# Moving a form's sums to GpSimd and fetching its blocks ahead in a Strassen decoder layer

## The chip, the cores and the metric

The kernel runs on one core of one Trainium2 chip. The metric is the device time of one execution in microseconds (us); less is better.

## The reference

One decoder layer, batch 1, 512 positions, width 2048, all in float32. Cut to what matters:

```python
h = rmsnorm(x, attn_norm_g)
proj = h @ w_in                       # u, v_sgu, q, k, v_att, g_a, g_b
y_a = chunked_spatial_gating(gelu(u), rmsnorm(gelu(v_sgu)), w_s, b_s)
y_b = stick_breaking_attention(rmsnorm(q), rmsnorm(k), v_att)
x = x + (sigmoid(g_a) * (y_a @ w_up_a) + sigmoid(g_b) * (y_b @ w_up_b)) @ w_o
h = rmsnorm(x, ffn_norm_g)
gate, up = split(h @ w_ffn_in)
x = x + (silu(gate) * up) @ w_ffn_out
x = x + sigmoid(rmsnorm(x, ple_norm_g) @ w_ple_gate) * (p @ w_ple)
```

The products with the weights w_in, w_up, w_o, w_ffn_in, w_ffn_out and w_ple_gate are nearly all of the work.

## The kernel before

Activations are kept transposed, 128 rows of the width (the partitions) by 512 positions. A float32 operand is split in two parts, `hi` (rounded) and `lo` (the rest), and `mm3` multiplies hi by hi, hi by lo and lo by hi. A unit of work multiplies a square of the weights (256 by 256, as four 128x128 blocks) with a raw block of activations of 128x1024 (256 rows of the width). It does so plainly ("P") or by Strassen's seven products ("S"), which need sums of weight blocks and of activation blocks.

*Weights.* Each group is fetched by the DMA queue of SyncE (SP). For "S" an accumulating DMA issued by GpSimd (POOL) adds two blocks in memory (`landed`, L317). Then ScalarE (ACT) writes the high part (`whi`, L313) and VectorE (DVE) the low part (L310), into three slots. Up to eight groups are fetched ahead, into `landings` that the low split gives back.

*Forms.* A form is the split operand of one raw block: `parts` is the arena of the split operands, `wholes` the arena of raw blocks, sums and landed weights. `split_into` is an ACT instruction (L245) and then a DVE instruction (L246). A late form (`late_form`, `plain_first`) first makes four sums of 128x256 on DVE (L464), t0 from two blocks, t1 from t0, t2 from t1, and one more, then splits blocks 0 to 3 (128x1024), a tick later the three sums (128x768, "3x256" below), and after its plain use the last (128x256), which overwrites a block. There are 34 late forms: 8 of the first input x, 8 of the feed-forward's input x1, 13 of the hidden layer, 5 of the gate's input x2. A first pass uses a form plainly, and later passes use it by Strassen. Where a norm's gain belongs to a form, `gained` (L451, two ACT instructions) scales the raw block first. x1, the hidden layer and x2 are spilled to HBM and loaded again by `load` (L447).

*Order.* Each engine runs its instructions in order. `tick`, called after each unit, takes the first form from the queue `builds` when it is `ready` and there is room, and runs its first step, which begins with the load; its further steps run one tick each through `after`. Instructions issued in a tick stand behind the unit's own on engines that have such. POOL's instructions have no such place and are put where the scheduler finds room.

*First stage and norms.* `ple_operands` loads and splits pT, and three products with w_ple (`ple_pair`, L766 copies the banks out) run first. Then each of the eight blocks of x (xT, L783) is multiplied plainly by three units (`w_first`). `Norm` squares each block (L831 on ACT, L835 on DVE), and at the end a chain of steps makes the row of 1/rms: a matmul, a power on POOL (L852), `spread` (four small matmuls, L819, on diagonals that DVE makes, L817) and a copy.

## Time and profile before

| | us |
|---|---|
| median of 3 runs | 2727.55 (2724.98 to 2731.51) |
| the profiled execution's own time | 2727.38 |
| its span | 2725.7 |
| PE busy | 2691.7 (99%) |
| DVE busy | 2073.5 (76%) |
| ACT busy | 1353.6 (50%) |
| POOL busy | 444.3 (16%) |

The mean granted clock of TensorE (PE) was 0.996 of full speed. Busy times of different engines overlap and do not add up. Lines such as L464 are line numbers of the kernel before, also where the text speaks of the kernel after; only in the rows of the order below the kernel after has its own line numbers.

### The profile page before, as it was taken

The page shows a single profiled execution, that of the slowest core. Times are in us where ns is not written, and L with a number is a line of the kernel's source. Part 1 is how long each engine was busy: PE and PEld are TensorE (multiplying, and loading weights), DVE is VectorE, ACT ScalarE, POOL GpSimd, SP SyncE. Part 2 cuts the span into 40 slices and gives each one's busy share as a digit, 9 for nine tenths or more (in the row PEclk, how much of TensorE's full clock was granted, in tenths as well). Part 3 has the DMA queues.
Part 4 walks back from the last instruction along what each step waited for, and adds up shares of the span by engine and source line. Part 5 has one row for each costly group of instructions (what it writes and reads, how often), then busy time and mean ns, then how long its engine had stood idle before and what let it go on. Part 6 is the DMA issues. An engine that isn't in the chain of part 4 may idle for free.

```text
span 2725.7 us, 45769 instructions
## 1 busy us (share of the span) xinstructions
PE 2691.7 (99%) x17243; PEld 2442.4 (90%) x17243; DVE 2073.5 (76%) x3375; ACT 1353.6 (50%) x2043; POOL 444.3 (16%) x527
## 2 busy tenths in 40 slices
PE   8999999999999999999999999999999999999999
PEld 6899999999999889978888888888888998988898
DVE  7666767667777657668989898989898667778776
ACT  7655555555554334365444444444445344454543
POOL 0222223222220000001111111111111101111110
PEclk9999999999999999999999999999999999999999
DMA  7667676677776447767888878887887668788785
GB/s 220 157 175 172 174 177 170 166 174 191 172 193 207 135 138 203 199 206 200 210 205 199 209 201 206 203 202 204 204 199 211 178 179 237 197 251 237 224 222 156
DMA packets 302846, 529.05 MB, mean 194 GB/s; under 512 B 25632, under 2 KB 162848, under 8 KB 302624
## 3 DMA queue, kind: packets, MB, share of 16 engines
q1 hardware_dynamic: 241872, 425.70, 49.3%
q0 software_dynamic: 60752, 100.43, 23.6%
q8 instruction: 135, 2.21, 0.3%
q14 instruction: 87, 0.71, 0.1%
HBM read 478.84 MB, written 47.19 MB: 193 GB/s over the span
## 4 chain that ended last, share of the span: by engine, by line
PE 87%; DVE 5%; DMA 4%; ACT 2%; issue 1%; POOL 1%; SPq 0%; ACTq 0%; DVEq 0%; POOLq 0%
PE ps L251 18%; PE ps L252 18%; PE ps L250 18%; PE ps L589 17%; PE ps L591 9%; PE small L589 3%; DVE wlo L310 1%; PE small L591 1%; DMA wholes<-x 1%; DMA wholes<-w_ffn_out 1%; DVE parts L246 1%; DVE wholes L464 1%; PE small L1011 1%; PE small L987 1%; PE small L964 1%
## 5 line engine op out<-in xcount | busy, mean ns | idle before, releaser
L250 PE MATMUL ps<-parts,whi 128*128 128x256 f32 (+1 forms) x3995 | 1247.2, 314 | 19.4 <-ACT whi L313 10.8
L313 ACT ACTIVATE whi<-wholes 128x512 fp32r<-128x512 f32 (+4 forms) x950 | 855.6, 917 | 801.1 <-PE ps L251 330.5
L251 PE MATMUL ps<-parts,whi 128*128 128x256 f32 (+1 forms) x3960 | 1232.9, 311 | 3.0 <-DVE parts L246 3.0
L252 PE MATMUL ps<-parts,wlo 128*128 128x256 f32 (+1 forms) x3960 | 1231.1, 311 | 3.2 <-DVE wlo L310 3.0
L310 DVE TENSOR_TENSOR wlo<-wholes,whi 128x512 fp32r<-128x512 f32 (+4 forms) x950 | 964.4, 1048 | 147.1 <-ACT whi L313 145.8
L250 PEld LDWEIGHTS ps<-parts,whi 128*128 128x128 f32 x3995 | 763.9, 191 | 68.8 <-ACT whi L313 12.1
L251 PEld LDWEIGHTS ps<-parts,whi 128*128 128x128 f32 x3960 | 758.1, 191 | 49.0 <-DVE parts L246 6.2
L252 PEld LDWEIGHTS ps<-parts,wlo 128*128 128x128 f32 x3960 | 757.8, 191 | 42.9 <-DVE wlo L310 4.6
L589 PE MATMUL ps<-parts,whi 128*128 128x512 f32 x2064 | 725.3, 391 | 0.0
L591 PE MATMUL ps<-parts,wlo 128*128 128x256 f32 x2064 | 578.8, 280 | 0.0
L589 PEld LDWEIGHTS ps<-parts,whi 128*128 128x128 f32 x2064 | 386.7, 187 | 83.7
L591 PEld LDWEIGHTS ps<-parts,wlo 128*128 128x128 f32 x2064 | 390.3, 189 | 0.1
L329 DVE TENSOR_TENSOR wholes<-wholes 128x256 f32<-128x256 f32 (+1 forms) x794 | 328.0, 413 | 24.3 <-DMA wholes<-w_ffn_out 4.9
L317 POOL DMA_DIRECT2D wholes<-w_ffn_in x172 | 149.7, 871 | 746.2 <-DMA wholes<-w_ffn_in 246.0
L317 POOL DMA_DIRECT2D wholes<-w_in x132 | 118.7, 903 | 548.7 <-DMA wholes<-w_in 226.8
L649 DVE TENSOR_TENSOR out<-out,ps 128x256 f32<-128x256 f32 x258 | 107.3, 416 | 78.6 <-ACT out L646 78.6
L618 DVE TENSOR_TENSOR out<-out 128x256 f32<-128x256 f32 x59 | 25.0, 425 | 175.9 <-ACT out L615 175.6
L246 DVE TENSOR_TENSOR parts<-wholes,parts 128x1024 fp32r<-128x1024 f32 (+3 forms) x129 | 122.9, 963 | 23.5 <-ACT parts L245 23.3
L589 PE MATMUL small<-parts,whi 128*128 128x512 f32 x344 | 128.8, 391 | 0.0
L245 ACT ACTIVATE parts<-wholes 128x1024 fp32r<-128x1024 f32 (+3 forms) x129 | 105.8, 845 | 40.8 <-DMA wholes<-hid 16.9
L317 POOL DMA_DIRECT2D wholes<-w_ffn_out x56 | 57.0, 1034 | 404.7 <-DMA wholes<-w_ffn_out 181.2
L1256 ACT ACTIVATE out<-out 128x512 f32<-128x512 f32 x44 | 27.9, 633 | 167.0 <-DVE out L1255 167.0
(119 smaller groups left out, 1659.1 us busy)
## 6 DMA issues: line engine op xcount, KB each, us to landing
wholes<-w_ffn_in SPq DMA_DIRECT2D x172, 384.0 KB, 5.5
wholes<-w_in SPq DMA_DIRECT2D x132, 384.0 KB, 4.8
wholes<-w_ffn_in SPq DMA_DIRECT2D x172, 256.0 KB, 4.7
wholes<-w_ffn_in POOLq DMA_DIRECT2D x172, 256.0 KB, 5.3
wholes<-w_in SPq DMA_DIRECT2D x132, 256.0 KB, 4.0
wholes<-w_in POOLq DMA_DIRECT2D x132, 256.0 KB, 4.7
wholes<-x SPq DMA_DIRECT2D x32, 512.0 KB, 5.3
wholes<-w_ffn_out SPq DMA_DIRECT2D x31, 512.0 KB, 4.0
```

The costliest lines, as they stand in the source:

```text
L245: return (nc.scalar.activation(hi, src, AF.Copy), nc.vector.tensor_tensor(out=lo, in0=src, in1=hi.bitcast(F32), op=ALU.subtract))
L246: nc.vector.tensor_tensor(out=lo, in0=src, in1=hi.bitcast(F32), op=ALU.subtract))
L250: nc.tensor.matmul(ps[:, s], sh, mh[:, s], start=start, stop=False)
L251: nc.tensor.matmul(ps, sh, ml, start=False, stop=False)
L252: return nc.tensor.matmul(ps, sl, mh, start=False, stop=stop)
L310: in_turn(nc.vector.tensor_tensor(out=self.lo[:, blocks], in0=r, in1=h.bitcast(F32), op=ALU.subtract))
L313: in_turn(nc.scalar.activation(h, r, AF.Copy))
L317: nc.gpsimd.dma_start(out=raw[:, 3:5], in_=self.src[:, 1:3], accum_op=ALU.add)
L329: in_turn(nc.vector.tensor_tensor(out=o, in0=x, in1=y, op=ALU.add))
L589: nc.tensor.matmul(ps, wh[:, w], t[:, x].rearrange("p s c -> p (s c)"), start=first, stop=False)
L591: mark(nc.tensor.matmul(ps[:, :256], wl[:, w], t[:, x, 0], start=False, stop=last))
L649: in_turn(nc.vector.tensor_tensor(out=out, in0=x, in1=y, op=op))
```

## The change

Four things are done together.

1. `plain_first` issues the split of blocks 0 to 3 ahead of the four sums, and the sums on POOL instead of DVE.
2. A form of a spilled block (`far`) can have its raw block loaded before its turn: `tick` looks at the first three forms of `builds` (AHEAD), and a form is not begun until two ticks (WAIT) after its load was asked for. Loads take the place in `wholes` that was given back longest ago ("old").
3. A norm's chain starts by itself after its eighth block, and three ticks lie between the power and `spread`. The two lines that ran the second and third norm's chains are gone.
4. pT is loaded and split in two halves behind the first w_ple, and `ple_pair` runs over the halves in the outer loop, with both banks open.

```diff
+AHEAD, WAIT = 3, 2
...
         last, units = traced()[-1], dict(newest)
-        if builds and builds[0].ready() and fits(builds[0].sizes):
+        for f in list(builds)[:AHEAD]:
+            if not f.there and f.ready() and fits([(wholes, 1024, "old"), (wholes, 1024, "low")]):
+                f.fetch()
+                break
+        if builds and builds[0].ready() and builds[0].arrived() and fits(builds[0].sizes):
             builds.popleft().step()
...
+        def fetch(self):
+            self.block, self.there, self.due = self.src(), True, clock[0] + WAIT
+            self.sizes = self.sizes[:-1]
+
+        def arrived(self):
+            return self.there and clock[0] >= self.due
...
-        b, s, v = cut(raw.f()), take(768), take(256)
+        b, s, v = cut(raw.f()), take(768, "old"), take(256, "old")
         t, x = cut(s.f()), form.operand()
+        split_into(x[:, 0:4, 0], x[:, 0:4, 1], b)
         for out, p, q, op in ((t[:, 0], b[:, 1], b[:, 0], ALU.subtract),
                               (v.f(), b[:, 1], b[:, 3], ALU.subtract),
                               (t[:, 1], t[:, 0], b[:, 3], ALU.subtract),
                               (t[:, 2], t[:, 1], b[:, 2], ALU.add)):
-            nc.vector.tensor_tensor(out=out, in0=p, in1=q, op=op)
-        split_into(x[:, 0:4, 0], x[:, 0:4, 1], b)
+            nc.gpsimd.tensor_tensor(out=out, in0=p, in1=q, op=op)
...
-        raw = load(pT)
-        hi, lo = parts.take(1024, "high"), parts.take(1024, "high")
-        split_into(hi.own(), lo.own(), raw.f())
+        raw = take(1024, "old")
+        ps_p.extend(parts.take(1024, "high") for _ in range(2))
+        for k in (0, T):
+            nc.sync.dma_start(out=raw.f(k, k + T), in_=pT[:, k : k + T])
+            split_into(*(x.own(k, k + T) for x in ps_p), raw.f(k, k + T))
...
+    w_ple_0 = plain_weights(w_ple[0])
     ple_operands()
-    ple_pair(0, False)
+    ple_pair(0, w_ple_0)
...
                 self.chain = Staged(self.steps())
+                self.chain.go_on()
...
-            yield
+            for _ in range(3):
+                yield
             ps = spread(self.cols)
...
-    after(3, norm2.chain.step)
...
-    norm3.chain.step()
```

The DMA queue of SP at the start of the program, before: one load of pT, two blocks of xT, and the third block (the next L783) behind the first prefetches of w_in.

```order
L447 DMA wholes_74<-pT 128x1024
L293 DMA wholes_74<-w_ple 128x512
L789 DMA gcol_110<-gains 128x58
L293 DMA wholes_74<-w_ple 128x512 x2
L293 DMA wholes_74<-w_first 128x512
L783 DMA wholes_74<-xT 128x1024 x2
L293 DMA wholes_74<-w_first 128x512 x3
...
L295 DMA wholes_74<-w_in 128x2x256 x3
L783 DMA wholes_74<-xT 128x1024
L293 DMA wholes_74<-w_first 128x512 x2
L783 DMA wholes_74<-xT 128x1024
```

The same queue after (L314 is a weight load, L785 half of pT, L819 a block of xT):

```order
L314 DMA wholes_74<-w_ple 128x512
L785 DMA wholes_74<-pT 128x512 x2
L819 DMA wholes_74<-xT 128x1024
L826 DMA gcol_113<-gains 128x58
L314 DMA wholes_74<-w_ple 128x512 x2
L314 DMA wholes_74<-w_first 128x512
L819 DMA wholes_74<-xT 128x1024 x2
...
L314 DMA wholes_74<-w_first 128x512
L819 DMA wholes_74<-xT 128x1024 x2
L314 DMA wholes_74<-w_first 128x512 x2
L316 DMA wholes_74<-w_in 128x2x256
```

Three blocks of xT stand ahead of the first result's store, and five ahead of the first w_in.

ACT in the first stage, from the last high split of the first block of x on, before (L313 high splits, L245 splits of a form, L831 squares, L451 gains):

```order
L313 ACTIVATE whi2_80<-wholes_74 128x512
L245 ACTIVATE parts_73<-wholes_74 128x4x256
L831 ACTIVATE out_16_178<-wholes_74 128x1024
L313 ACTIVATE whi0_76<-wholes_74 128x512
L831 ACTIVATE out_19_204<-wholes_74 128x1024
L313 ACTIVATE whi1_78<-wholes_74 128x512
```

The same place after (L334 high splits, L266 splits of a form, L868 squares, L483 gains):

```order
L266 ACTIVATE parts_73<-wholes_74 128x4x256
L868 ACTIVATE out_16_181<-wholes_74 128x1024
L334 ACTIVATE whi2_80<-wholes_74 128x512
L483 ACTIVATE wholes_74<-wholes_74,gcol_113 128x512
L868 ACTIVATE out_21_209<-wholes_74 128x1024
L483 ACTIVATE wholes_74<-wholes_74,gcol_113 128x512
L868 ACTIVATE out_23_222<-wholes_74 128x1024
L266 ACTIVATE parts_73<-wholes_74 128x4x256
L334 ACTIVATE whi0_76<-wholes_74 128x512
L266 ACTIVATE parts_73<-wholes_74 128x3x256 x2
L334 ACTIVATE whi1_78<-wholes_74 128x512
```

The gains, the square and the split of the third block of x now stand ahead of whi0, the high split of the second block's first weights, and two splits of 3x256, which wait for POOL, ahead of whi1.

POOL from w_o to the first weights of w_ffn_out, before: it issues accumulating DMAs (L317) and one power.

```order
L317 DMA wholes_74<-w_o 128x512 x16
L317 DMA wholes_74<-w_ffn_in 128x512 x2
L852 TENSOR_TENSOR cols_918_11846<-mean_917_11844,expo_121 128x4
L317 DMA wholes_74<-w_ffn_in 128x512 x170
L317 DMA wholes_74<-w_ffn_out 128x512 x2
L317 DMA wholes_74<-w_ffn_out 128x2x128
```

The same stretch after, its last part (L338 accumulating DMAs, L497 sums):

```order
L338 DMA wholes_74<-w_ffn_in 128x512 x8
L497 TENSOR_TENSOR wholes_74<-wholes_74 128x256 x4
L338 DMA wholes_74<-w_ffn_in 128x512 x8
L497 TENSOR_TENSOR wholes_74<-wholes_74 128x256
L338 DMA wholes_74<-w_ffn_in 128x512 x136
L338 DMA wholes_74<-w_ffn_out 128x512
L497 TENSOR_TENSOR wholes_74<-wholes_74 128x256 x7
L338 DMA wholes_74<-w_ffn_out 128x512
L338 DMA wholes_74<-w_ffn_out 128x2x128
L497 TENSOR_TENSOR wholes_74<-wholes_74 128x256 x9
```

The sums of the first three hidden-layer forms stand among the DMAs of w_ffn_in, 136 of them ahead of the stage that uses them; the others follow the first DMA of w_ffn_out.

More of the change, by code (lines that the diff above doesn't have):

```diff
@@ L221, in step, with go_on @@
                     after(1, self.step)
+        def go_on(self):
+            if not self.going:
+                self.going = True
+                after(1, self.step)
         def get(self):
@@ L406, in __init__, with raw @@
             self.blocks, self.at_plain, self.used = None, kind == "P", False
+            self.src, self.there, self.block, self.due = src, not far, None, 0
+        def fetch(self):
[3 more added lines that the diff above has]
+            return self.there and clock[0] >= self.due
+        def raw(self):
+            return self.src() if self.block is None else self.block
         def get(self):
@@ L432, in use_plain @@
             self.used = True
-            if not self.done:
-                after(1, self.step)
+            self.go_on()
         def free(self):
@@ L487, in steps @@
             return form.operand()
-        return Form("S", steps, [(parts, 2 * PLACE, "place")] + [(wholes, 1024, "low")] * 2, ready)
+        return Form("S", steps, [(parts, 2 * PLACE, "place")] + [(wholes, 1024, "low")] * 2, ready,
+                    src, far)
     def strassen_form(src, ready=always, gain=None, raw=PLACE):
```

62 lines of the change are left out of this document (36 added, 26 removed).

## The prediction

> **What bounds the kernel now.** I read the page's busy times first, then TensorE's (PE's) waits, then a table of short windows with the granted clock, and last the timelines of PE, ScalarE (ACT) and the DMA queue inside those windows. The first two, from the page and from the waits of PE (engine, line, what it waited for, us in total, times, longest):
>
> ```profile
> span 2725.7 us, 45769 instructions
> PE 2691.7 (99%) x17243; PEld 2442.4 (90%) x17243; DVE 2073.5 (76%) x3375; ACT 1353.6 (50%) x2043; POOL 444.3 (16%) x527
> ```
>
> ```profile
> PE ps L250 <- ACT whi L313: 10.8, 4, 6.3
> PE ps L250 <- ACT parts L245: 5.1, 4, 2.5
> PE ps L252 <- DVE wlo L310: 3.0, 4, 1.0
> PE ps L251 <- DVE parts L246: 3.0, 5, 0.8
> PE ps L250 <- ACT out L766: 2.9, 2, 1.7
> ```
>
> PE is the bound, and the change leaves its matmuls alone. All that can be won is time in which PE waits or runs slow. Its waits after the first matmul are 10.8 - 6.3 + 5.1 + 3.0 + 3.0 + 2.9 = 18.5 us, with about 3 us in shorter groups. That DVE is 76% busy costs nothing by itself. The windows that hold these waits (us from the start; busy time and count of PE, PEld, DVE, ACT, POOL; then PE's granted clock, DMA share, GB/s):
>
> ```profile
> 33.00:45.00 12.00, 7.89 (x23) 5.71 (x22) 9.65 (x18) 9.06 (x13) 0.00 (x0) 0.72 0.63 178
> 1200.00:1208.00 8.00, 5.09 (x21) 3.60 (x20) 6.31 (x9) 7.77 (x11) 0.00 (x0) 1.00 0.93 319
> 1224.00:1232.00 8.00, 6.15 (x20) 4.46 (x19) 6.95 (x15) 7.84 (x12) 1.73 (x2) 0.79 0.93 251
> 2081.00:2096.00 15.00, 12.52 (x52) 9.40 (x51) 14.33 (x22) 7.17 (x8) 2.16 (x2) 0.89 0.81 219
> 2259.00:2286.00 27.00, 23.72 (x154) 20.70 (x153) 20.61 (x35) 12.65 (x19) 2.95 (x3) 1.00 0.85 237
> 2554.00:2574.00 20.00, 16.15 (x76) 12.71 (x75) 15.03 (x28) 11.25 (x16) 2.92 (x3) 0.91 0.81 226
> ```
>
> PE's idle time in them is the width less its busy time: 4.1, 2.9, 1.9, 2.5, 3.3 and 3.9 us. A clock below 1.00 is a second loss behind a wait: 12 x 0.28 = 3.4 us in the first window, then 8 x 0.21 = 1.7, 15 x 0.11 = 1.7 and 20 x 0.09 = 1.8. PE's timeline gives the longest waits in them, and those of the start (start, duration, and in brackets the idle time before and what ended it):
>
> ```profile
> 6.28 0.80 PE L250 MATMUL ps<-parts,whi 128*128 128x512 f32 x1 [6.28 <-ACT whi L313]
> 38.41 0.79 PE L250 MATMUL ps<-parts,whi 128*128 128x512 f32 x1 [3.58 <-ACT whi L313]
> 93.04 0.49 PE L819 MATMUL small<-diag,ones 128*128 128x128 f32 x2 [0.78 <-DVE diag L817]
> 1202.99 0.51 PE L250 MATMUL ps<-parts,whi 128*128 128x512 f32 x1 [1.25 <-ACT out L766]
> 1207.70 0.50 PE L250 MATMUL ps<-parts,whi 128*128 128x512 f32 x1 [1.65 <-ACT out L766]
> 1226.48 0.73 PE L250 MATMUL ps<-parts,whi 128*128 128x512 f32 x2 [1.21 <-ACT parts L245]
> 2090.02 0.73 PE L250 MATMUL ps<-parts,whi 128*128 128x512 f32 x2 [1.22 <-ACT parts L245]
> 2285.05 0.39 PE L252 MATMUL ps<-parts,wlo 128*128 128x256 f32 x1 [1.02 <-DVE wlo L310]
> 2557.56 0.73 PE L250 MATMUL ps<-parts,whi 128*128 128x512 f32 x2 [2.47 <-ACT parts L245]
> ```
>
> PE names ACT or DVE, but the chain goes one step further. ACT's own timeline, just ahead of those waits:
>
> ```profile
> 34.61 1.33 ACT L451 ACTIVATE wholes<-wholes,gcol 128x512 f32<-128x512 f32 x2 [2.80 <-DMA wholes<-xT]
> 1200.17 1.34 ACT L451 ACTIVATE wholes<-wholes,gcol 128x512 f32<-128x512 f32 x2 [3.43 <-DMA wholes<-x]
> 1224.00 1.34 ACT L451 ACTIVATE wholes<-wholes,gcol 128x512 f32<-128x512 f32 x2 [1.96 <-DMA wholes<-x]
> 2258.48 1.06 ACT L245 ACTIVATE parts<-wholes 128x1024 fp32r<-128x1024 f32 x1 [3.10 <-DMA wholes<-hid]
> 2555.09 1.34 ACT L451 ACTIVATE wholes<-wholes,gcol 128x512 f32<-128x512 f32 x2 [3.95 <-DMA wholes<-x]
> ```
>
> Each time ACT stands at the raw block of a form whose load was asked for too late, and the weights' high halves (whi, L313) and the bank copies (L766) queue behind that instruction. That is what fetching ahead takes away.
>
> **The change part by part.** The costs of one, from the grouped view (busy us, mean ns) and from the single lines of GpSimd (POOL; min/median/max ns):
>
> ```profile
> L464 DVE TENSOR_TENSOR wholes<-wholes 128x256 f32<-128x256 f32 x136 | 52.5, 419 | 12.4 <-ACT wholes L451 12.2
> L451 ACT ACTIVATE wholes<-wholes,gcol 128x512 f32<-128x512 f32 x42 | 28.2, 715 | 25.0 <-DMA wholes<-x 19.1 <-DMA wholes<-xT 5.9
> L831 ACT ACTIVATE out<-wholes 128x1024 f32<-128x1024 f32 x24 | 25.3, 1056 | 28.8 <-DVE wholes L1293 20.7 <-DVE wholes L694 7.8 <-DVE wholes L835 0.2
> L245 ACT ACTIVATE parts<-wholes 128x1024 fp32r<-128x1024 f32 x57 | 59.6, 1054 | 32.4 <-DMA wholes<-hid 16.9 <-DMA wholes<-pT 6.2 <-DMA wholes<-y 5.3
> L245 ACT ACTIVATE parts<-wholes 128x768 fp32r<-128x768 f32 x34 | 28.4, 836 | 6.0 <-DVE wholes L464 5.7
> L245 ACT ACTIVATE parts<-wholes 128x256 fp32r<-128x256 f32 x34 | 12.7, 404 | 2.4 <-PE ps L252 2.4
> L313 ACT ACTIVATE whi<-wholes 128x512 fp32r<-128x512 f32 x431 | 270.1, 627 | 232.9 <-DVE wholes L329 181.8 <-PE ps L251 25.5 <-issue 23.1
> ```
>
> ```profile
> L997 POOL COPY wholes<-wholes x24: 289/397/1427, 117.2 to 611.2; 128x128 f32<-128x128 f32 x24
> L1002 POOL TENSOR_SCALAR_AFFINE_SELECT wholes<-wholes x32: 292/700/1961, 125.7 to 624.3; 128x128 f32<-128x128 f32 x32
> ```
>
> *The sums.* 136 sums of 128x256 (34 forms, four each) leave DVE, which gives back 52.5 us there, nearly all in time PE does not wait for. On POOL this operation is not in the trace. The nearest rows are 128x128: 289 ns undisturbed and 1961 ns at worst, and 397 to 700 ns at the median. Per sum I take 1.0 us, twice the columns at a median between those two; the bounds are 0.29 and 1.96 us. The three steps that follow one another make 3 to 4 us per form, where DVE took 4 x 0.42 = 1.7. Who waits: ACT's split of three blocks (L245, 128x768) stands in order behind the last sum, and behind it on ACT stand the next whi splits and bank copies. What hides it: the split of blocks 0 to 3, which the plain pass needs, now goes ahead of the sums, and the raw block is there earlier. For the first three hidden-layer forms the sums stand on POOL among the weight DMAs of w_ffn_in, far before ACT needs them.
>
> By the Trainium skill, "GPSIMD Engine Reference", section 3.1, an add of two tensors takes GpSimd 1.96 times as long as VectorE: an estimate of 0.82 us here, and the sum would come out the same. "SBUF — State Buffer", Who interferes with whom, says that a DVE instruction with two SBUF inputs and a reading GpSimd instruction exclude each other for the whole instruction; 292 against 1961 ns for one shape agrees, and this speaks against the change.
>
> *First block in halves.* PE's first matmul waited 6.28 us for pT (512 KB) and its split. With w_ple first and half of pT (256 KB) split by a half-sized instruction (about 0.5 us less than the 1054 ns), I take 0.9 us off (0 to 1.5).
>
> *First stage.* The third block of xT is now asked for beside the first two, and the fourth ahead of the w_in prefetches. So the window's 4.1 us of idle time (the 3.58 us wait and a short one) and its slow clock go, 4.1 + 3.4 = 7.5 us. In return ACT has more to do before the second block's first weights: two L451, two L831 less the one it had, and a 1024 split, 2 x 0.72 + 1.06 + 1.05 = 3.6 us. It had 2.8 us free a little later, so some of it becomes a new wait: 2.5 us taken (1 to 6). Net -5.0.
>
> *Norm chain in steps.* The 0.78 us at 93.04 goes, with a little behind it: -0.9 (0 to 1). For the third norm the chain is no longer run ahead of the pass; it could cost as much there, and the pass's own matmuls cover it.
>
> *Forms for the feed-forward's input (1180 to 1232).* Idle 2.9 + 1.9 and 1.7 of clock are 6.5 us. ACT's 3.43 us wait goes, since that load is now given out ticks earlier. The last block cannot come much earlier, because it is stored just before: 1.5 stay. Net -5.0. ACT begins with these forms here:
>
> ```profile
> 1179.42 1.94 ACT L451 ACTIVATE wholes<-wholes,gcol 128x512 f32<-128x512 f32 x3
> ```
>
> From then to PE's wait at 1207.70 are 28 us, into which the sums of five forms fall, 20 us at 1.0 each.
>
> *Hidden-layer forms.* At 2081 to 2096 DVE is busy 14.33 of 15 us, so here the sums' leaving helps: idle 2.5 and 1.7 of clock are 4.2, I take -3.0, since the fourth and fifth forms' sums still stand behind the first accumulating DMA of w_ffn_out. At 2259 to 2286 several short waits make 3.3 us: -2.5.
>
> *Gate forms (2554 to 2574).* Idle 3.9 and 1.8 of clock are 5.7. The 3.95 us wait of ACT goes; the sums add a little: -4.0.
>
> *Sum.* -0.9 - 5.0 - 0.9 - 5.0 - 3.0 - 2.5 - 4.0 = -21.3. Against it I set 3 us for ACT standing behind POOL's sums at the places where POOL is also issuing weights (half of the forms, some 0.2 us each that reaches PE): -18.3. The profiled execution took 2727.38 us (span 2725.7), the median of the runs is 2727.55: 2709.
>
> Where a clock loss is counted, the Trainium skill, "TensorE: Matmul & The Clock Gate", Part 1, gives an idle window of about 3.4 us before the rate halves; here waits of 1.21, 1.22 and 2.47 us too are followed by slow windows (0.79, 0.89, 0.91), so the trace disagrees. By that rule the three smaller clock losses would not belong to the waits, and the time would be some 5 us higher.
>
> **Rivals.**
> *Slower: ACT stands behind POOL.* If DVE's long two-input instructions block most sums, one costs up to 1.96 us. In the first stage a form's work on ACT that cannot overlap the sums is 1.43 + 0.84 + 0.40 (the 256 split) + 1.25 (two whi) = 3.9 us, and PE needs a form every 36 matmuls (three units of twelve). One starts every 0.23 us, as two neighbours of that stage show:
>
> ```profile
> 13.44 0.39 PE L252 MATMUL ps<-parts,wlo 128*128 128x512 f32 x1
> 13.67 0.39 PE L250 MATMUL ps<-parts,whi 128*128 128x512 f32 x1
> ```
>
> That is 8.2 us a form, so from (8.2 - 3.9)/4 = 1.1 us a sum on, each form is late: at 1.96, 3.5 us by five forms, 17 us. At 1179 twenty sums take 39 us where there are 28: 11 more. With 3 at the hidden layer that is +31 on -18: 2740. It decides from about 1.6 us a sum. For it: L1002's longest. Against: the medians 397 and 700, and DVE is less loaded just there.
>
> *Less won: bandwidth, not order.* At 1200 and 1224 the DMA share is 0.93. If an earlier raw block only delays the weights and the stores in the same queue, the 5.0 and 4.0 of the feed-forward's and the gate's inputs are lost: 2718. Against it: 0.63 at 33 to 45 and 0.81 at 2554.
>
> *Nothing.* The new waits of the first stage (6 us) and of the later forms (12) eat the gain: 2727. That the loads do not move at all is excluded by the order of the DMA queue.
>
> *All of it.* Every wait counted goes: 7.5 + 0.9 + 0.9 + 6.5 + 4.2 + 3.3 + 5.7 = 29: 2698.
>
> **How the numbers follow.** Forecast 0.52, less won 0.16, all of it 0.06 (together faster, 0.74), nothing 0.10, slower 0.16. A difference of 0.2% (5.5 us) is about what a measurement of this kernel can tell from none. The range runs from 2699, where nearly all waits go, to 2732: the rest of the slower case, about one in ten, and of the best, one in twenty, stay outside.
>
> **What would show it.** Right: the 3.58, 1.65 and 2.47 us waits of PE and ACT's waits for wholes<-xT and wholes<-x gone, the clock at 1.0 in 33 to 45, POOL's sums at 0.6 to 1.2 us each, and about 50 us less busy DVE. Wrong: ACT's 768 splits waiting long for POOL wholes, sums over 1.6 us, or PE waiting for whi between 20 and 70 us with a low clock. If the sums are short and the waits stay, the loads were not the cause.

## The result, and the profile after

The changed kernel took 2746.77 us (median of 4 runs, 2744.86 to 2756.15) against 2727.86 (4 runs, 2724.98 to 2731.51): a ratio of 1.0068, 95% interval 1.0051 to 1.0086. The forecast was 2709 with a range up to 2732, so its sign was wrong. A second set of runs had the same kernel at 2759.5, 1.0117 (1.0102 to 1.0132). The profiled execution took 2756.15 us, 28.8 more than the one before. Line numbers in the rows of the kernel after are its own: L497 the sums, L266 and L267 the split of a form, L331 and L334 the split of weights, L271 to L273 the three products of `mm3` (L250 to L252 before), L483 the gains, L556 the low part of a plain form, L623 and L625 the pair of matmuls of the feed-forward's input (512 and 256 columns; L589 and L591 before), L872 the sum of squares of a norm, L882 its matmul; L942 is a transposition behind the first norm, and L964 the ACT instruction that it waits for. The page and PE's waits (us in total, times, longest):

```profile
span 2754.4 us, 45796 instructions
PE 2710.6 (98%) x17243; PEld 2444.0 (89%) x17243; DVE 2083.0 (76%) x3241; ACT 1354.1 (49%) x2045; POOL 600.9 (22%) x663
```

```profile
PE ps L273 <- DVE wlo L331: 13.2, 11, 2.5
PE small L882 <- DVE wholes L872: 9.3, 2, 7.4
PE ps L271 <- ACT parts L266: 8.0, 3, 5.2
PE small L942 <- ACT wholes L964: 2.5, 1, 2.5
PE ps L272 <- DVE parts L267: 1.8, 2, 1.1
```

Before, PE waited for ACT; now it waits mostly for DVE. And DVE, which gave away 136 additions of 52.5 us, is 9.5 us busier than before (2083.0 against 2073.5). What it still does takes about 62 us longer. The groups (busy us, mean ns; idle before and its cause):

```profile
L497 POOL TENSOR_TENSOR wholes<-wholes 128x256 f32<-128x256 f32 x136 | 157.2, 1206 | 167.1 <-ACT wholes L483 100.5 <-DVE parts L267 27.1 <-DMA sum<-wholes 20.0
L267 DVE TENSOR_TENSOR parts<-wholes,parts 128x1024 fp32r<-128x1024 f32 x55 | 79.7, 1456 | 12.0 <-ACT parts L266 12.0
L267 DVE TENSOR_TENSOR parts<-wholes,parts 128x768 fp32r<-128x768 f32 x34 | 37.8, 1114 | 13.6 <-ACT parts L266 13.6
L266 ACT ACTIVATE parts<-wholes 128x768 fp32r<-128x768 f32 x34 | 28.6, 841 | 47.5 <-POOL wholes L497 47.4
L483 ACT ACTIVATE wholes<-wholes,gcol 128x512 f32<-128x512 f32 x42 | 28.1, 711 | 6.5 <-DMA wholes<-x 5.6 <-DMA gcol<-gains 0.9
```

In the last row 25.0 us of ACT's waiting for raw blocks became 6.5. That fetching ahead did it isn't shown: without any fetch ahead (the first group below) the same row has 6.4, and with POOL's sums alone in the kernel before 22.1. Something else of the change, such as loads into the places given back longest ago, is enough; it was not run alone. The two rows, without fetches ahead and with the sums alone:

```profile
L483 ACT ACTIVATE wholes<-wholes,gcol 128x512 f32<-128x512 f32 x42 | 28.3, 711 | 6.4 <-DMA wholes<-x 5.5 <-DMA gcol<-gains 1.0
```

```profile
L451 ACT ACTIVATE wholes<-wholes,gcol 128x512 f32<-128x512 f32 x42 | 28.3, 715 | 22.1 <-DMA wholes<-x 14.6 <-DMA wholes<-xT 6.7 <-DVE wlo L310 0.7
```

The L266 row of the changed kernel shows what came instead, 47.4 us of ACT standing at POOL's sums. The gate forms show the worst place. DVE's timeline, then POOL's, then PE's (start, duration, idle time before):

```profile
2581.26 0.75 DVE L556 SCALAR_TENSOR_TENSOR parts<-wholes,gcol,parts 128x512 fp32r<-128x512 f32 x1
2581.92 0.69 DVE L872 TENSOR_TENSOR wholes<-wholes,out 128x512 f32<-128x512 f32 x1
2582.53 3.25 DVE L556 SCALAR_TENSOR_TENSOR parts<-wholes,gcol,parts 128x512 fp32r<-128x512 f32 x1
2585.70 1.70 DVE L872 TENSOR_TENSOR wholes<-wholes,out 128x512 f32<-128x512 f32 x1
```

```profile
2582.64 2.58 POOL L497 TENSOR_TENSOR wholes<-wholes 128x256 f32<-128x256 f32 x3
...
2585.68 1.16 POOL L497 TENSOR_TENSOR wholes<-wholes 128x256 f32<-128x256 f32 x1
```

```profile
2587.45 1.87 PE L882 MATMUL small<-ones,wholes 128*128 128x1 f32 x8 [7.37 <-DVE wholes L872]
```

One form of instruction takes DVE 0.75 us, and 3.25 us while three sums run on POOL beside it; the next takes 1.70 in place of 0.69. Of PE's 7.37 us, these two make 3.5 (2.50 and 1.01). The sums themselves, min/median/max in ns:

```profile
L497 POOL TENSOR_TENSOR wholes<-wholes x136: 720/1154/9406, 9.5 to 2585.7; 128x256 f32<-128x256 f32 x136
```

A second loss is no wait. In the feed-forward's input PE is busy throughout, before and after, and yet it starts fewer matmuls in the same 650 us (width, busy PE and its count, then PEld, DVE, ACT, POOL, granted clock, DMA share, GB/s). Before, and after:

```profile
1410.00:2060.00 650.00, 650.00 (x3751) 573.89 (x3751) 580.15 (x1042) 312.05 (x435) 113.98 (x131) 1.00 0.81 202
```

```profile
1410.00:2060.00 650.00, 650.00 (x3681) 563.69 (x3680) 568.31 (x1021) 306.82 (x427) 115.55 (x131) 1.00 0.81 201
```

650 us over 3751/2 pairs is 346.6 ns a pair, over 3681/2 it is 353.2, at a granted clock of 1.00 in both. The stage has 2408 such pairs, in 43 units, so the difference over all of it is 2408 x 6.6 ns = 16 us. In this execution the first four units, up to 1325 us, still ran at 347, so that 39 x 56 x 6.6 ns = 14 us of it were lost. Below, the two are called 347 and 353.

### The profile page after: what moved, and what is told of

It is laid out like the page before. It is cut to its first block, busy times and chain, and to the rows that moved or that the text cites. A ratio compares the mean times of both kernels' runs of the same rounds, so it can differ in the third digit from the quotient of the medians.

```text
span 2754.4 us, 45796 instructions
## 1 busy us (share of the span) xinstructions
PE 2710.6 (98%) x17243; PEld 2444.0 (89%) x17243; DVE 2083.0 (76%) x3241; ACT 1354.1 (49%) x2045; POOL 600.9 (22%) x663
## 4 chain that ended last, share of the span: by engine, by line
PE 87%; DVE 4%; DMA 3%; POOL 2%; issue 2%; ACT 1%; SPq 0%; POOLq 0%; DVEq 0%; ACTq 0%
PE ps L273 18%; PE ps L272 18%; PE ps L271 18%; PE ps L623 17%; PE ps L625 9%; PE small L623 3%; POOL wholes L497 2%; PE small L625 1%; DVE wlo L331 1%; DVE parts L267 1%; DMA wholes<-w_ffn_out 1%; DMA wholes<-x 1%; PE small L942 1%; PE small L1050 1%; PE small L1026 1%
## 5 line engine op out<-in xcount | busy, mean ns | idle before, releaser
L271 PE MATMUL ps<-parts,whi 128*128 128x256 f32 (+1 forms) x3995 | 1247.0, 314 | 8.9 <-ACT parts L266 8.0
L273 PE MATMUL ps<-parts,wlo 128*128 128x256 f32 (+1 forms) x3960 | 1231.5, 311 | 13.4 <-DVE wlo L331 13.2
L334 ACT ACTIVATE whi<-wholes 128x512 fp32r<-128x512 f32 (+4 forms) x950 | 855.4, 916 | 790.2 <-PE ps L272 303.0
L331 DVE TENSOR_TENSOR wlo<-wholes,whi 128x512 fp32r<-128x512 f32 (+4 forms) x950 | 978.7, 1064 | 160.2 <-ACT whi L334 158.0
L271 PEld LDWEIGHTS ps<-parts,whi 128*128 128x128 f32 x3995 | 764.2, 191 | 56.9 <-ACT parts L266 8.9
L273 PEld LDWEIGHTS ps<-parts,wlo 128*128 128x128 f32 x3960 | 757.4, 191 | 56.5 <-DVE wlo L331 18.6
L623 PE MATMUL ps<-parts,whi 128*128 128x512 f32 x2064 | 738.3, 398 | 1.1 <-DVE out L683 0.5
L625 PE MATMUL ps<-parts,wlo 128*128 128x256 f32 x2064 | 579.2, 281 | 0.0
L623 PEld LDWEIGHTS ps<-parts,whi 128*128 128x128 f32 x2064 | 387.7, 188 | 98.3 <-issue 1.9
L625 PEld LDWEIGHTS ps<-parts,wlo 128*128 128x128 f32 x2064 | 389.8, 189 | 0.0
L338 POOL DMA_DIRECT2D wholes<-w_ffn_in x172 | 151.8, 883 | 666.0 <-DVE wholes L350 268.8
L338 POOL DMA_DIRECT2D wholes<-w_in x132 | 117.8, 892 | 486.5 <-DMA wholes<-w_in 205.3
L497 POOL TENSOR_TENSOR wholes<-wholes 128x256 f32<-128x256 f32 x136 | 157.2, 1206 | 167.1 <-ACT wholes L483 100.5
L267 DVE TENSOR_TENSOR parts<-wholes,parts 128x768 fp32r<-128x768 f32 (+4 forms) x131 | 144.7, 1119 | 31.8 <-ACT parts L266 31.8
L266 ACT ACTIVATE parts<-wholes 128x768 fp32r<-128x768 f32 (+4 forms) x131 | 105.7, 834 | 69.3 <-POOL wholes L497 47.4
L623 PE MATMUL small<-parts,whi 128*128 128x512 f32 x344 | 131.0, 398 | 0.0
L338 POOL DMA_DIRECT2D wholes<-w_ffn_out x56 | 57.6, 1052 | 283.5 <-DMA wholes<-w_ffn_out 94.5
```

Of the source, the lines that this page charges most:

```text
L267: nc.vector.tensor_tensor(out=lo, in0=src, in1=hi.bitcast(F32), op=ALU.subtract))
L271: nc.tensor.matmul(ps[:, s], sh, mh[:, s], start=start, stop=False)
L273: return nc.tensor.matmul(ps, sl, mh, start=False, stop=stop)
L331: in_turn(nc.vector.tensor_tensor(out=self.lo[:, blocks], in0=r, in1=h.bitcast(F32), op=ALU.subtract))
L334: in_turn(nc.scalar.activation(h, r, AF.Copy))
L338: nc.gpsimd.dma_start(out=raw[:, 3:5], in_=self.src[:, 1:3], accum_op=ALU.add)
```

## The experiments

They ran in five groups; each has its own runs of the kernel before (medians 2727.0, 2727.7, 2727.3, one run of 2727.0, and 2728.4 in this order).

**First group: which of the four parts costs it.**

*The changed kernel again.*

> The kernel after, unchanged, a second time. Its first profile showed the 512-column matmuls of the feed-forward's first part starting every 236 ns, where the kernel before has 230, on the same operand addresses (2408 of them, 14 us), and that execution took 2756 where its fellows took 2745 to 2747. If the slower pace belongs to the program, the second profile has a median near 236 again. If it is a chance of the execution, the median is 230 in this profile, the span is near 2744, and the change alone costs 17 to 20 us, in the waits. Time 2743 to 2748 in both cases.

2759.5 us (2756.85 to 2763.21, 4 runs), ratio 1.0117 (1.0102 to 1.0132); the wait at the third norm is 7.3 us again, and so is the slow pace, but for two stretches at 347 (1289 to 1325 and 1369 to 1405 us). The time was expected at 2743 to 2748. It was 13 us above the first set of runs. The pace could be the reason: in that set the profiled execution, mostly at 353, took 2756 where the others took 2745 to 2747. But no profile of those others exists, so it is not shown.

*The sums back on DVE, all else kept.*

```diff
-            nc.gpsimd.tensor_tensor(out=out, in0=p, in1=q, op=op)
+            nc.vector.tensor_tensor(out=out, in0=p, in1=q, op=op)
```

> The kernel after with the four sums back on DVE, still behind the split; all else kept. Theory POOL (the sums' 1.2 us each, and DVE standing still while a GpSimd sum holds what both share, are the loss): the waits of ACT for sums (47 us) and of PE for the low halves of weights (13 us) go, and the time falls by 12 to 16 us, to 2731 or below. Theory NORM (the third norm's matmuls stand in PE's order ahead of their data, 7.4 us) and theory FETCH (early loads push weights back): the time falls by less than 5 us, to 2741 or more.

2733.09 us (11 runs), 1.0017 (1.0007 to 1.0027): 26.4 us less than the changed kernel beside it, so POOL's sums make the sign, and yet no gain is left. In its groups DVE's splits are short again:

```profile
L267 DVE TENSOR_TENSOR parts<-wholes,parts 128x1024 fp32r<-128x1024 f32 x55 | 66.8, 1219 | 5.1 <-ACT parts L266 5.1
L497 DVE TENSOR_TENSOR wholes<-wholes 128x256 f32<-128x256 f32 x136 | 52.2, 418 | 4.0 <-ACT wholes L483 3.9
```

Now count, over the whole trace, how much later each matmul starts behind the last one than is usual for their two sizes, wherever that is over 0.1 us (a slow clock behind a wait counts too). This is 58 us before, 80 in the second profile of the changed kernel, and 46 here. By waits alone this version should be 12 us faster than the kernel before. Its pairs ran at 353 from end to end, which took that back.

*The norm chains as before* (`go_on` and the three steps out, the two chain calls back).

> The kernel after with the norm chains started as in the kernel before (second and third by their own lines, one tick between power and spread). Theory NORM: the 7.4 us wait of PE at the third norm's sums goes, and with the 2.5 us at the first norm the time falls by 7 to 10 us, to 2737 to 2740. Theory POOL: PE's wait at the third norm is DVE held up by four GpSimd sums, and would come back at another place; the time falls by less than 4 us.

2759.61 us (6 runs), 1.0112 (1.0094 to 1.0129), no different from the changed kernel. In its profile (2753.65 us) the pairs ran at 347 from 1411 us on, and yet it took 26 us more than the profiled execution before: the pace is not all of the loss. The third norm still waits, so its cause isn't that the chain starts by itself:

```profile
2585.10 1.87 PE L881 MATMUL small<-ones,wholes 128*128 128x1 f32 x8 [7.48 <-DVE wholes L872]
```

*No form fetched ahead.*

```diff
-            self.src, self.there, self.block, self.due = src, not far, None, 0
+            self.src, self.there, self.block, self.due = src, True, None, 0
```

> The kernel after without loads ahead of a form's turn (no form is far; the old order of arena places is kept). Theory FETCH: what PE waits for between 2390 and 2490 (6 us) is caused by early loads and goes, time 2738 to 2742. Theories POOL and NORM: those waits stay, and the gains at 2081 to 2096 and 2259 to 2286 (together 6 us) are lost, so the time rises to 2750 or more.

2756.85 us (6 runs), 1.0101 (1.0083 to 1.0119): 2.7 us under the changed kernel, within what its own runs spread. With POOL's sums in place the fetches ahead win nothing. ACT stands at the sums for 40.0 us here; that this is the reason was not tested.

**Second group: does POOL's work cost because somebody waits for it, or because DVE stands beside it; and what redraws the pace.**

*The sums on DVE, and besides four additions of the same blocks on POOL into a tile that nobody reads.*

```diff
+        for p, q in ((1, 0), (1, 3), (3, 2), (2, 0)):
+            nc.gpsimd.tensor_tensor(out=spare_sum, in0=b[:, p], in1=b[:, q], op=ALU.add)
```

> The kernel after with the four sums made on DVE, and beside them four GpSimd additions per form of the same size on the same raw block, into a block that nobody reads (they add work and leave none out). Nobody waits for a GpSimd sum, but DVE meets it. Theory LOCK (DVE stands still while a reading GpSimd addition runs; that delays the low halves of weights and the bank sums): most of the 26 us between the kernel after and the one with sums on DVE comes back, 2748 to 2760. Theory LATENCY (ACT's split of three blocks waits for the sums, and whi queue behind it): the time stays near 2733, at most 2739.

2790.52 us (5 runs), 1.0230 (1.0212 to 1.0249), 57 us above the same kernel without them, which ran in the first group. No instruction reads their result; one wait is on record for them, 3.5 us of ACT. Its page and groups:

```profile
PE 2718.9 (98%) x17243; PEld 2450.2 (88%) x17243; DVE 2135.4 (77%) x3377; ACT 1352.8 (49%) x2045; POOL 605.2 (22%) x663
```

```profile
L499 POOL TENSOR_TENSOR spare_sum<-wholes 128x256 f32<-128x256 f32 x136 | 163.5, 1203 | 127.9 <-ACT wholes L483 73.1 <-issue 28.9 <-DMA wholes<-hid 17.6
L497 DVE TENSOR_TENSOR wholes<-wholes 128x256 f32<-128x256 f32 x136 | 78.7, 613 | 3.4 <-ACT wholes L483 3.3
```

DVE's own sums go from 418 to 613 ns and its whole busy time from 2073.1 to 2135.4. So additions on POOL cost DVE time, and the kernel too, without anybody using their result. The Trainium skill, "SBUF — State Buffer", Who interferes with whom, says that of a DVE instruction with two SBUF inputs and a reading GpSimd instruction one blocks fully; the 3.25 and the 613 agree with that. Not all of the 57 us came through DVE. PE's longest wait in this run, then POOL ahead of it:

```profile
2164.40 0.58 PE L271 MATMUL ps<-parts,whi 128*128 128x256 f32 x1 [8.44 <-ACT whi L334]
```

```profile
2127.61 18.69 POOL L499 TENSOR_TENSOR spare_sum<-wholes 128x256 f32<-128x256 f32 x4 [4.03 <-DMA wholes<-hid]
2146.24 0.91 POOL L338 DMA_DIRECT2D wholes<-w_ffn_out  x1
2146.85 7.30 POOL L499 TENSOR_TENSOR spare_sum<-wholes 128x256 f32<-128x256 f32 x7
2154.10 0.86 POOL L338 DMA_DIRECT2D wholes<-w_ffn_out  x1
```

The accumulating DMAs of the weights stood behind the additions in POOL's order, and ACT waited 15.8 us for such weights. Across this place the run lost 12 us on the version without the additions. How the rest divides between DVE and the engines behind it was not told apart, and neither was it for the 26 us of the changed kernel, where PE's waits for high parts (`whi`) come to 0.5 us only.

*The sums on DVE and the norm chains as before.*

> The kernel after with the sums on DVE and the norm chains as in the kernel before: loads ahead and the first block in halves are what is left. The first norm lost 3.7 us in the profile with sums on DVE and 1.7 in that with the old norm chain, so 2730 to 2732 if that is all; above 2735 if the steps help the third norm.

2733.1 us (12 runs), 1.0014 (1.0000 to 1.0028), the same as without that edit: in sum the norm chains weigh nothing either way. With the changed chains PE waits 2.4 us behind the first norm (for ACT L964), with the old ones 1.9 us there and 4.1 us for the second norm's diagonals.

*A pause in the kernel before,* and *the same in the version with the sums on DVE:*

```diff
+        if m == 2:
+            for _ in range(16):
+                in_turn(nc.vector.tensor_tensor(out=tri, in0=ones, in1=ident, op=ALU.add))
```

> The kernel before with 16 useless additions of 128x128 on DVE (4.5 us) in the third unit of the feed-forward's first part, which hold PE for 1 to 4 us once. Theory PACE (the interval of the matmul pairs there is drawn anew when PE has waited, 347 or about 354 ns, and kept until it waits again): the pairs run at 347 ns up to the hold and may run at 354 from there, which would cost up to 16 us more, 2728 to 2731 or 2740 to 2748. Without PACE: 2728 to 2731, and 347 ns throughout.

> The kernel after with the sums on DVE and the same hold. In its profile the pairs ran at 354 ns from the first to the last. Theory PACE: the hold can set them to 347 ns, which gives 2720 to 2722, or leave them at 354, 2735 to 2738. Without PACE: 2735 to 2738 and 354 ns throughout.

2742.97 us (4 runs, 1.0051, 1.0035 to 1.0068) and 2731.11 (10 runs, 1.0014, 1.0004 to 1.0025). In the first the pairs were at 353 even ahead of the pause, at 347 for 16 us between two halts of PE, and at 353 behind it; in the second at 353, for 30 us at 347 to 349, and at 353 again. In these two runs the pace stayed between halts of PE, and changed at halts, in either direction. They didn't show what decides.

**Third group: POOL's sums alone, the order of sums and split, and where the pace comes from.**

*POOL's sums, behind the split, in the kernel before.*

> The kernel before with one part of the change alone: the four sums of a late Strassen form on GpSimd, with the split of the raw block ahead of them; fetches, norm chains and the first block as before. LOCK (while GpSimd adds, the DVE operation beside it stands still, so 136 sums cost DVE and what waits for it): the sums alone cost most of the loss; against the kernel before 20 to 35 us slower (2748 to 2762), of which up to 15 us is the pace of the matmul pairs of the ffn_in stage if this program draws the 353 ns pace, and a wait of several us at the matmul of the third norm near 2580. REST (the sums are harmless by themselves, and the loss comes from the fetches, the norm chains and the halves): within 5 us of the kernel before, 2723 to 2733.

2785.73 us (2765.53 to 2787.84, 6 runs), 1.0188 (1.0161 to 1.0215): 58 us slower, more than the whole change, and more than was expected of it. The other three parts thus do win beside POOL's sums: 26 us by the second set of the changed kernel, 40 by the first.

*The sums on DVE, ahead of the split, as before; the rest stays changed.*

> The changed kernel with the sums on VectorE and ahead of the split, as in the kernel before; fetches, norm chains and the first block stay changed. ORDER (with the sums on VectorE, the split ahead of them delays the sums that the first matmuls of a form need, and that is what is left of the loss): the waits for the parts of x1 and of the hidden forms fall, and the time is 5 us or more under the kernel with the split ahead (2733), 2718 to 2728. PACE (what is left of the loss is the pace of the ffn_in pairs, 353 ns against 347): the time stays within 4 us of 2733 when its pairs run at 353 ns, and comes to 2713 to 2720 when they run at 347.

2736.2 us (6 runs), 1.0028 (1.0017 to 1.0039): the order of sums and split isn't the cause (ORDER falls); pairs at 353 throughout.

*The same, the norm chains as before, and the x1 forms not fetched ahead.*

> As the kernel with the sums on VectorE ahead of the split, and besides with the norm chains of the kernel before and with no fetch ahead for the eight x1 forms, so that TensorE comes into the ffn_in stage as in the kernel before; the first block in halves, the earlier x and the fetches ahead for the hidden, x2 and y forms stay. ENTRY (the pace of the ffn_in pairs is drawn by how TensorE enters the stage): 347 ns pairs, and the gains of the first stage (3 to 5 us) and of the hidden and gate forms (4 to 9 us) show: 2714 to 2722. IMAGE (the pace goes with the program as a whole, whatever its entry): 353 ns pairs in most programs that are not the kernel before, 2727 to 2736.

2732.32 us (11 runs), 1.0017 (1.0008 to 1.0025), pairs at 353. ENTRY in the form given there (an entry like that of the kernel before brings 347) was not borne out: PE came into this stage without a halt.

*The kernel before, with 16 useless additions far behind the stage.*

> The kernel before with 16 useless 128x128 additions on VectorE in the fifth pair of the last stage (near 2650 us), far behind the ffn_in stage, in slack that VectorE has there (16 of about 0.3 us each, some 5 us of VectorE). ENTRY (the pace is set by what runs up to the stage): as the kernel before, 2724 to 2731 in most runs with 347 ns pairs. IMAGE (the pace goes with the program): 353 ns pairs and 2738 to 2744, although nothing ahead of or in the stage is changed.

2726.76 us (11 runs), 0.9991 (0.9982 to 1.0001), and the stage as before:

```profile
1410.00:2060.00 650.00, 650.00 (x3751) 573.13 (x3751) 580.18 (x1042) 312.33 (x435) 114.59 (x132) 1.00 0.82 202
```

So the pace doesn't go with the program as a whole (IMAGE falls). The starts of the pairs, taken from the trace, say more. At 347 the intervals from one 512-column matmul to the next are even (347, 347, 346) or alternate (350, 343); at 353 they repeat in threes (350, 361, 349). Six versions that run through the stage's first pairs without a halt (the four so far with the sums on DVE and no pause, the one without fetches ahead, the one with the old norm chains) all start with 340, 350, 361, 349. The changed kernel ran at half clock just ahead of the stage, and started at 347 in its first profile and at 353 in its second. The kernel before halts just behind the first pair (1.0 us between two starts, here 1.9) and goes on at 347. With the pause in it, it halted there for 0.88 us and went on at 353; with an extra matmul far behind that place (the last run of the fifth group) it halted for 0.88 us too and went on at 347. So the length of the halt alone doesn't decide.

**Fourth group: a shift of the matmuls by themselves.** One short extra matmul ahead of a unit's first pair (a unit is 56 pairs), with `c` columns and into the bank that the pair then overwrites:

```diff
+                        if first and i == 0:
+                            nudges[0] += 1
+                            c = (0, 32, 64, 96, 128, 160, 192, 224)[0 if not nudges[0] else 1 + (nudges[0] - 1) % 7]
+                            if c:
+                                nc.tensor.matmul(ps[:, :c], wh[:, w], t[:, x, 0][:, :c],
+                                                 start=True, stop=True)
```

> The changed kernel with the sums on VectorE ahead of the split (2736), and with one short extra matmul ahead of the first pair of each of the 43 doubled units of the ffn_in stage but the first: 32, 64, 96, 128, 160, 192 and 224 columns in turn, into the bank that the pair then overwrites; some 3 us of TensorE in all. PHASE (the pace of the pairs, 347 or 353 ns, is set by how TensorE's matmuls fall against each other, and stays until something shifts them): the pace changes at units' borders, and the size of the extra matmul decides which pace follows, so that units behind the same size agree; if half of them come to 347 ns, the stage is 8 us shorter, less the 3: near 2731. OUTSIDE (something outside TensorE, set at the entry, holds the pace): all 43 units keep 353 ns, and the time is 2736 and the 3 us of the extra matmuls, 2739.

2739.01 us (one run, beside 2726.95 of the kernel before). The pace changes at units' borders, and units of one size that come from the same pattern do the same: in five of the six units behind 64 columns the pattern is that of 353 for nine pairs and that of 347 behind them; in five of six behind 96 columns it turns to 353; four of six behind 128 columns are at 347 from end to end (the next expectations count a fifth, which falls to 353 at its tenth pair). PHASE holds; OUTSIDE, that all 43 stay at 353, falls. Sorted by the pace that the unit before had, the map says more: 64, 96, 128 and 160 columns changed the pace, to whichever was the other, in 23 of 24 units, and 32, 192 and 224 left it in 17 of 18. The extra matmul thus swaps the two paces rather than choosing one, and the four runs of the fifth group agree.

**Fifth group: one such matmul, in the second unit alone** (`c = 128 if nudges[0] == 1 else 0`; 96 in the last).

*In the version with the sums on DVE ahead of the split* (2736 without):

> The changed kernel with the sums on VectorE ahead of the split (2736), and with a single extra matmul of 128 columns ahead of the second doubled unit of the ffn_in stage, 0.12 us of TensorE. PHASE (the fall of the matmuls against each other holds until something shifts it; in the map of the extra matmuls, 128 columns behind a unit of 353 ns gave 347 to 348 ns for the whole unit in five cases of six): 42 units of 56 pairs come from 353.3 to 346.7 ns, 15.5 us less: 2718 to 2724. NOT KEPT (the pace falls back to 353 ns at the next unit's border or by some other disturbance): 2728 to 2737.

2730.87 us (2717.7 to 2734.28, 12 runs), 1.0005 (0.9995 to 1.0016), above the 2718 to 2724 of PHASE. In its profile (2725.79 us) the pairs are at 347 from 1249 to 1581 us; there one pair comes 0.1 us late, and from it on they are at 353.

*In the version with the sums on DVE behind the split* (2733 without):

> The changed kernel with the sums on VectorE behind the split (2733), with the same single extra matmul of 128 columns. PHASE: 15.5 us less than without it: 2715 to 2721, against 2727 of the kernel before, so a version faster than both kernels; it would show what the parts of the change other than GpSimd's sums are worth: 6 to 12 us. NOT KEPT: 2726 to 2735.

2723.89 us (2714.94 to 2729.42, 12 runs), 0.9976 (0.9963 to 0.9990), 3 us above what PHASE gave. Its profiled execution, at 347 to the end of the stage, took 2716.89 us:

```profile
1410.00:2060.00 650.00, 650.00 (x3751) 568.38 (x3750) 580.25 (x1039) 314.62 (x438) 113.55 (x131) 1.00 0.82 203
```

*In the version that also has the norm chains as before and no x1 form fetched ahead* (2732 without):

> The version with the sums on VectorE ahead of the split, the norm chains of the kernel before and no fetch ahead for the x1 forms (2732), with the same single extra matmul of 128 columns. PHASE: 2714 to 2721. NOT KEPT: 2725 to 2735.

2715.28 us (2714.26 to 2722.95, 6 runs), 0.9958 (0.9944 to 0.9973): faster than both kernels. Its profiled execution took 2720.99: a pair that came 0.3 us late at 1950 us put the last 116 us of the stage at 353.

*In the kernel before, 96 columns:*

> The kernel before with a single extra matmul of 96 columns ahead of the second doubled unit of the ffn_in stage, 0.1 us of TensorE; in the map, 96 columns behind a unit that ran at 347 to 348 ns turned it to 353 ns in five cases of five. PHASE: 42 units at 353.3 in place of 346.7 ns, 15.5 us more: 2738 to 2744 for 0.1 us of added work. NOT KEPT, or the pace comes from elsewhere: 2724 to 2731 as the kernel before.

2742.17 us (2737.41 to 2748.06, 6 runs), 1.0050 (1.0037 to 1.0064): 13.8 us for one matmul of 0.1 us. The first unit of doubled pairs still has 347, the second loses it, and the rest is as in the kernel after:

```profile
1410.00:2060.00 650.00, 650.00 (x3681) 563.63 (x3680) 569.25 (x1019) 306.78 (x425) 114.92 (x132) 1.00 0.81 200
```

The intervals show in the timeline too (the first and the seventh start of a 512-column matmul in the same 2 us; before, then with the extra matmul):

```profile
1699.63 0.39 PE L589 MATMUL ps<-parts,whi 128*128 128x512 f32 x1
...
1701.71 0.39 PE L589 MATMUL ps<-parts,whi 128*128 128x512 f32 x1
```

```profile
1699.65 0.40 PE L596 MATMUL ps<-parts,whi 128*128 128x512 f32 x1
...
1701.77 0.40 PE L596 MATMUL ps<-parts,whi 128*128 128x512 f32 x1
```

Six pairs take 2.08 and 2.12 us.

## Why the prediction was wrong

*The account.* Three terms, each from its own pair of kernels: POOL's sums +26.4 us (the changed kernel against the one with the sums on DVE); the pace +13.8 (the kernel before with and without the one extra matmul); the other parts together -10.5 (the profiled execution of the version with the sums on DVE and 347 pairs, 2716.89, against 2727.38). They add up to +29.7; measured were +18.9 in the first set, +32.5 in the second and +28.8 between the profiled executions.

*Stage by stage.* All these programs run the same 17243 matmuls (the extra one left out). So a stage's gain or loss is how far the same matmul, counted from the program's start, comes earlier or later behind the stage than ahead of it. In us, minus is won; the stages by the times of the kernel before, each version by its profiled execution. The kernel before with 16 additions near its end differs from the kernel before by up to 1.2 us in a row. The forecast's allowance of 3 us has no place of its own.

| stage | forecast | changed kernel | sums on DVE | the same, pairs at 347 |
|---|---|---|---|---|
| start and first stage, to 85 | -5.9 | +0.9 | -6.4 | -6.4 |
| first norm, to 120 | -0.9 | +3.9 | +3.8 | +2.6 |
| to 1178 | 0 | +1.1 | +1.2 | +1.4 |
| x1 forms, to 1237 | -5.0 | +2.7 | -5.1 | -5.4 |
| pairs of the feed-forward's input, to 2070 | 0 | +16.8 | +16.4 | +0.6 |
| hidden forms, to 2286 | -5.5 | -6.3 | -3.7 | -3.8 |
| to 2554 | 0 | +6.4 | -0.1 | +2.4 |
| gate forms and third norm, to 2585 | -4.0 | +3.5 | -2.6 | -1.6 |

With the sums on DVE the terms of the first stage and of the x1 forms came as forecast; with the sums on POOL they were gone. The norm's term was wrong in each.

*The sums: the step that failed.* Their length was taken at 1.0 us and came to 1.206 (median 1.154, 720 ns at the least), within its bounds. The 0.82 us that the prediction estimated from the Trainium skill, "GPSIMD Engine Reference", section 3.1, is nearer to the shortest. But the step counted the 52.5 us as given back by DVE and looked for who waits on the sums only through ACT's split. The prediction had the row for it (one shape on POOL at 292 and 1961 ns) and read it as a price to POOL alone. DVE pays as well: 62 us over the program, and the largest waits are now PE's on DVE. The 3 us allowance for ACT behind POOL was the wrong entry, and too small.

*The slower rival* had the right sign, place and cause in its condition (DVE's long instructions and the sums blocking each other), but priced it by ACT's queue, from 1.6 us a sum on. At 1.2 us a sum it should not have come about; the loss came all the same, since DVE's delay doesn't need a late sum. Its 2740 missed the 2747 by less than the forecast, and its chance of 0.16 was too low.

*Third norm.* The prediction let the pass's own matmuls cover the chain. PE waited 7.37 us there; with the old chain 7.48. With the sums on DVE it is 1.17. So cover was gone because of POOL's sums, which held DVE at 2582, not because of the order; the 3.5 us shown above are half of it, and the rest was not followed. *First norm:* -0.9 forecast; PE's wait at 93 went, one of 2.5 us at 110 came, and 3.9 us were lost. With the old chain the changed kernel loses nothing there (-0.3).

*First stage.* -5.0 forecast. The 3.58 us wait went and the clock in 33 to 45 is 1.00, as said. The new waits, feared on ACT, are five on DVE's low parts of the weights (0.36 to 1.78 us each). In the window 24 to 62 PE is busy for 33.89 us before, 32.20 in the changed kernel, and 36.58 with the sums on DVE:

```profile
24.00:62.00 38.00, 33.89 (x138) 27.18 (x137) 31.42 (x58) 27.82 (x41) 2.67 (x3) 0.91 0.68 199
```

```profile
24.00:62.00 38.00, 32.20 (x128) 24.23 (x127) 37.79 (x36) 29.78 (x44) 26.68 (x26) 0.96 0.68 191
```

```profile
24.00:62.00 38.00, 36.58 (x159) 29.28 (x158) 35.78 (x63) 30.45 (x47) 3.71 (x4) 1.00 0.74 212
```

*x1 and gate forms.* ACT's wait for the raw block is gone in both, as forecast (though, as said, not shown to go by fetching ahead), and PE gained nothing, since it then waited for DVE (1.47 us at 1204) and for the norms (1.89 us at 1213, 7.37 us). At 1204 DVE itself had stood 2.33 us at ACT, and ACT 2.99 us at POOL's sums. *Hidden forms:* right. The changed kernel runs the matmuls of 2081 to 2096 from 2106.5 on and those of 2259 to 2286 from 2282.1 on, in 12.1 us where it took 15.0 and in 23.1 where it took 26.5, so 2.8 and 3.5 us were won against 3.0 and 2.5 forecast:

```profile
2106.52:2118.64 12.12, 11.41 (x51) 9.16 (x50) 12.12 (x18) 6.44 (x8) 8.59 (x2) 1.00 1.04 345
2282.12:2305.17 23.05, 22.25 (x153) 20.64 (x152) 16.75 (x26) 10.35 (x16) 7.37 (x8) 1.00 0.98 292
```

As much was given back later, 6.4 us up to the gate forms: waits of 2.28 us for ACT and 1.41 and 2.54 for DVE between 2430 and 2491.

*First block in halves.* -0.9 forecast; the first matmul starts at 5.22 in place of 6.28 us, 1.06 won, but the 17th, at 12 us, already comes 0.2 us later than before.

*What no step held.* "PE is the bound, and the change leaves its matmuls alone" took the matmuls' own pace as fixed. It was not: the same pairs on the same operands cost 347 or 353 ns by how they fall against each other, and the six versions that ran through the stage's first pairs without a halt all started at 353. That is worth 13.8 us, more than the x1, hidden and gate terms of the forecast less the allowance (5.0 + 3.0 + 2.5 + 4.0 - 3.0 = 11.5).

*What stays open.* Why the pairs lock into one of the two patterns, why the changed kernel ran 13 us apart in two sets of runs, and which part of the change took ACT's waits for raw blocks away. Whether the version at 2715 can be held at 347 in every run wasn't tried.

## What to carry to other kernels

Work moved off a busy engine onto GpSimd isn't free for the engine it leaves: when both read two operands in SBUF, price each GpSimd instruction as time that VectorE may stand, too, try it with a dummy that nobody waits for, and see what stands behind it in GpSimd's own order. When a version removes waits and the time doesn't follow, count the matmuls in equal windows of a stage in which TensorE never waits: the count tells a change of pace that no busy time and no wait shows. Where a long, stall-free stage has such paces, one short extra matmul at its start is a cheap trial.

## What was not expected of the hardware

- A pair of 512 and 256 columns, each behind its own weight load, runs at 346.6 or 353.2 ns, at a granted clock of 1.00. The Trainium skill, "TensorE: Matmul & The Clock Gate", Back-to-back issue gap, says that the spacing in such a stream is set by both operations; here the same two operations had two spacings.
- One extra matmul of 0.1 us moved a program by 13.8 us, and one pair that was 0.1 us late undid such a shift. Of 42 extra matmuls of 32 to 224 columns in one execution, those of 64 to 160 swapped the pace in 23 of 24 cases, and the others kept it in 17 of 18.
- A DVE instruction of 0.75 us took 3.25 us beside three sums on POOL, and one sum on POOL took 9.4 us behind DVE's instructions (720 ns at the least).
